# A depthwise convolution in two half-width phases, VectorE in program order during the attention, and later LayerNorms and weights, in a one-core encoder step

## The chip, the core and the metric

The kernel runs on one core of a Trainium2 chip. Of that core it uses TensorE (matrix products), VectorE, ScalarE and GpSimd (elementwise work; GpSimd also starts transfers that add to their target) and SyncE, which starts most transfers. The page of the profile calls them PE, DVE, ACT, POOL and SP; PEld is TensorE's loading of weights. The metric is the time of one execution on the chip in microseconds (us), smaller is better, given as the median of several runs.

## The reference, cut to what matters

One step of a hybrid encoder layer for 1040 prompt tokens (16 learned ones and 1024 frames) and 32 tokens of a running stream, all in float32.

```python
glu, q, k, v = project(rmsnorm(x, norm_mix), w_in)      # glu = a * sigmoid(b), 512 channels
glu_ext = concat([conv_state, glu])                     # 30 earlier rows in front
y = depthwise_causal_conv(glu_ext, dw_w, dw_b)          # 31 taps for each channel, plus bias
a_out = silu(layernorm(y) * ln_g + ln_b)                # over the 512 channels
attn = chunked sliding-window attention(q, k, v, bias, sinks)
x = x + concat([a_out, attn]) @ w_out
x = x + conv_ffn(x)                                     # up, 3 taps, swish gate, down
return rmsnorm(x), caches
```

The convolution at issue is, for every channel c and token t, y[t, c] = bias[c] + sum over k from 0 to 30 of w[k, c] * glu_ext[t + k, c].

## The kernel before, in words

**Layout.** Channels lie on the 128 partitions and tokens run along the free dimension. The 1072 tokens are worked in three token blocks, b = 0, 1, 2 (TB, OB: 336 or 324, 384 and 352 columns). The 512 convolution channels are four channel blocks, p = 0 to 3. `glu[:, p]` holds the convolution's input, `acc[:, p]` its output (ACCW = 1102 columns, with a gap between prompt and stream). A product in full precision is made of three matmuls, with each operand split into a rounded high part and a residue (`mm3`, L252 to L257); `split` (L248 to L250) makes the high part with a cast on ScalarE and the residue with a subtraction on VectorE. `wsplit` (L237) does it for weights.

**Order of the work.** 
1. Input projections for all columns but the last channel block (`in_group`, L646); `in_evac` (L566) puts the results into place on VectorE, gating included.
2. The loop of the attention (L1007 to L1042), 20 steps: a job enters per step (1 for the learned tokens, 16 chunks, and the stream's at step 12). In a step, the job that entered the step before gets its softmax finished (`soft_b`, L767: a reciprocal and four multiplications, of which the last SCA[i] run on ScalarE, L774, and the others on VectorE, L772); the new job gets its scores (TensorE), bias and maximum (`softmax_a`, L757, VectorE) and exponentials (L764, ScalarE); then come the outputs of the job before last (`outs`, L837), the transposes of the last one (`trans`, L821), its copies (`probs`, L828) and `keep` (L845). FILL[i] pieces of the last channel block's projection fill the step (`stream`; 48 pieces, 7 done ahead of the loop). When they are through, `after_glu` (L942) splits the attention's result, two channel groups at a time (`ca_split`, L931), and the first matmuls of the attention's half of the output projection are made (`ahs`). For the two entries in CSD, `ca_split` makes the residues not on VectorE but as a negated copy on ScalarE (L936) and a transfer of GpSimd's that adds the source to it.
3. The attention's half of the output projection: 20 groups of 12 matmuls (L1118 to L1135). After every third matmul comes a `tick` (L1095), which drives the three LayerNorms (`ln`, L1050, one for each token block): the first starts at tick LN0 = 14, each next one LNS = 21 ticks after the one before it started, if no tap that it needs is left. In `ln`, `squared` notes that its sum of squares is through. After the group in which all three are noted, `open_cv` (L1108) opens the buffers CVH and CVL, and the LayerNorms may go on to their last step, the split into them (L1084 to L1087). If that has not come about by the end of the groups, L1136 to L1140 finish it there.
4. The rest of the convolution half's weights (L1141 to L1143), and `conv_half` (L1155) for each token block: eight outputs, each of 12 matmuls, added to X by VectorE (L1165), squared and split.
5. The feed-forward part, from L1203 on, which the change doesn't touch.

**The taps.** When a channel block's columns are there, `taps_of` (L616) puts a convolution into the queue `tapq`, one entry for each segment in SEGS: blocks 1 and 2 are one segment each of all three token blocks (1090 columns), block 0 is two, block 3 is three, one for each token block. An entry is 31 instructions on VectorE (`conv_taps`, L395 to L410): one multiplication with the bias added (the profile has it at L400) and 30 that multiply and add (L403). `taps(us)` (L434) takes taps from the queue, from its first two entries in turn (WAYS = 2), and charges each (columns + 120) / 960 us until the budget is used. In the attention the budget of step i is TA[i]; in phase 3 it is TH = 5.9 for each group.

**What sets the order.** In the regions `tc.manual_schedule(engines=MANUAL)` TensorE and ScalarE run their instructions in the order of the program. All other engines' orders come from a planner that simulates the timeline; taps are issued in `tc.high_priority(offset=-1000000)`, so that everything else goes ahead of them, and behind the instruction named in `issue_after` (in the attention, the last score operation of the step). MANEND is MANUAL with VectorE and is used at the kernel's end.

Of the kernel before, what the change touches and what calls it, by code (L numbers as in the profile page):

```python
# [11 lines left out]
F32 = mybir.dt.float32  # L12
# [39 lines left out]
NPB = 8  # L52
TGS = [3.0, 3.0, 1000.0, 1000.0]
TGW = [3.0, 5.0, 6.5, 3.5, 1000.0, 1000.0, 5.0, 1000.0, 1000.0, 1000.0, 3.5, 3.5, 1000.0, 1000.0, 1000.0, 1000.0, 1000.0, 1000.0, 3.0, 3.0, 1000.0, 1000.0, 1000.0, 1000.0, 1000.0, 1000.0, 7.0, 3.5, 3.5, 3.5]
TA = [2.01, 2.74, 5.63, 6.64, 4.22, 3.28, 2.42, 2.68, 2.08, 1.57, 2.08, 2.08, 3.18, 1.41, 2.1, 0.85, 4.71, 3.21, 5.98, 2.57]
TH = 5.9
WAYS = 2
BS = ((0, 2), (1, 0), (2, 1), (2, 2))
# [11 lines left out]
WLD = True  # L70
MANUAL = {mybir.EngineType.PE, mybir.EngineType.Activation}
MANEND = MANUAL | {mybir.EngineType.DVE}
SCA = [1, 2, 2, 2, 1, 1, 2, 2, 2, 2, 2, 1, 2, 2, 0, 1, 1, 2, 2, 2]
LN0 = 14
LNS = 21
FILL = [4, 6, 6, 2, 3, 3, 6, 1, 3, 3, 1, 4, 5, 0, 3, 6, 0, 3, 0, 3]
ORDER = [2, 3, 8, 9, 4, 5, 10, 11, 12, 13, 6, 7]
CHAINS = ((0, 1),)
# [2 lines left out]
CHK = 21  # L81
CHT = 0
CHG = (1, 2)
SEGS = (((0,), (1, 2)), ((0, 1, 2),), ((0, 1, 2),), ((0,), (1,), (2,)))
CSD = ['12', '00']
AH = (1, 2, 1, 3, 5, 4, 5)
AG = (('00', '02'), ('h',), ('l',), ('10',), ('12',))
AT = (1, 8)
# [81 lines left out]
def body(nc, tc, cp, wp, xp, dp, io):  # L170
# [22 lines left out]
    def pcol(name, i):  # L193
        o, _ = PRM[name]
        return prm[:, o + i:o + i + 1]
# [196 lines left out]

    tapq, spare = [], [0.0, 0]

    def conv_taps(p, a0, a1, b):  # L395
        e, a = glu[:, p, :], acc[:, p, a0:a1]

        def tap(k):
            if k == 0:
                nc.vector.tensor_scalar(out=a, in0=e[:, a0:a1], scalar1=pcol("cw", p * CW), scalar2=pcol("cb", p),  # L400
                                        op0=ALU.mult, op1=ALU.add)
            else:
                nc.vector.scalar_tensor_tensor(out=a, in0=e[:, a0 + k:a1 + k], scalar=pcol("cw", p * CW + k),  # L403
                                               in1=a, op0=ALU.mult, op1=ALU.add)

        ks = list(range(CW))
        if (p, b) in CHAINS:
            ks = [0, *range(CHK, CW)]
            chq.append([p, a0, a1, list(range(1, CHK))])
        tapq.append([b, a1 - a0, tap, ks, p])  # L410
# [225 lines left out]
    def flush():  # L636
        undefer()
        while pend and pend[0][1] in ready:
            c, b, ps = pend.pop(0)
            if c % 2:  # L640
                undefer()
            in_evac(c, b, ps)
            if c < 8 and c % 2:
                taps_of(c // 2, b)
# [54 lines left out]
    def fetch():  # L699
        if wsrc:  # L700
            raws.append(wraw(wsrc.pop(0)))
# [302 lines left out]
    left = (len(order) - NPRE) * 3 * KD - PF  # L1004
    for _ in range(PF):
        next(stream)
    for i in range(len(jobs) + 2):  # L1007
        job = jobs[i] if i < len(jobs) else None
        if a:
            a.soft_b(SCA[i])  # L1010
        if job:
            job.scores()
            job.soft_a()
            job.exps(0)
            job.exps(1)
        if z:
            z.outs()
        if a:
            a.trans()
            a.probs()  # L1020
        if z:
            z.keep()
            kept[0] = i - 2
        for _ in range(min(FILL[i], left)):
            next(stream)
            left -= 1
        flush()
        taps(TA[i], (job or a or z).q[1][3])
        if not left and not pend and not defer:
            for _ in stream:  # L1030
                pass
            next(later, None)
            ticks = len(jobs) + 2 - i
            for _ in range(AH[-ticks] if ticks <= len(AH) else 0):
                next(ahs, None)
            for q in adds:
                ah_add(*q)
            adds.clear()
        if i == CHE:
            with tc.issue_after(job.q[1][3]):  # L1040
                chain_end()
        z, a = a, job  # L1042
    for _ in later:
        pass
    for _ in ahs:
# [90 lines left out]
    if not CVH:  # L1136
# [1 line left out]
        while len(squared) < 3:  # L1138
            tick()
        open_cv()  # L1140
    for m2 in WOC[1:]:  # L1141
        whl[m2] = halves(take((None, None, *wres)[m2], WLD))
        fetch()  # L1143

    close(cS)
    cH, ph = pool("h3", "right")
# [8 lines left out]
    def conv_half(b, rms):  # L1155
        t0, n = OB[b]
        at = t0 - H0
        for i, m in enumerate(2 * h + j for h in WOC for j in range(2)):
            hi, lo = whl[m // 2][m % 2]
            ps = mmt()[:, :n]  # L1160
            for k in range(4):
                mm3(ps, [k], lambda k: hi[:, k, :], lambda k: lo[:, k, :], lambda k: CVH[b][:, k, :],
                    lambda k: CVL[b][:, k, :], k == 0, k == 3)
                tick()
            nc.vector.tensor_tensor(out=X[b][:, m, :], in0=X[b][:, m, :], in1=ps, op=ALU.add)  # L1165
            sq_sum(X[b][:, m, :], rb[b][:, :n], acc[:, i % 4, t0:t0 + n], i, nc.gpsimd)
            gsplit(BH[:, m, at:at + n], BL[:, m, at:at + n], X[b][:, m, :], pcol("g2", m))
            if i % 2:
                nc.sync.dma_start(xd[:, m - 1:m + 1, at:at + n], X[b][:, m - 1:m + 1, :])
            if rms and i in RS:  # L1170
                next(rms)
        for _ in rms or ():
            pass
# [724 lines left out]
```

## Time and profile before

| what | value |
|---|---|
| median of 3 runs | 1048.87 us (1048.4 to 1048.88) |
| the profiled execution | 1049.94 us |
| its span | 1048.2 us |
| instructions | 19994 |
| mean TensorE clock granted | 0.999 |

The profile is of one execution. Its page lists busy times, a chain of the work that ended last, and groups of instructions by line. The views beside it answer from the same trace: the waits of an engine (who waited, who released it, total, how often, the longest), busy time in stretches of time, and a timeline (start in us, how long the row lasts, engine, line, operation, output and inputs, size, how many instructions the row joins; in brackets the idle time before it and who ended it). Consecutive instructions of a kind are one row. The matmuls' ends are modelled, and they overlap, so a matmul's time is not its pace.

| stage | from to (us) |
|---|---|
| attention loop | 163.8 to 248.4 |
| attention's half of the output projection | 248.4 to 293.1 |
| first matmul of the convolution half | 293.1 |

### The profile page before, as it was taken

The page shows a single profiled execution, that of the slowest core. Times are in us where ns is not written, and L with a number is a line of the kernel's source. Part 1 is how long each engine was busy: PE and PEld are TensorE (multiplying, and loading weights), DVE is VectorE, ACT ScalarE, POOL GpSimd, SP SyncE. Part 2 cuts the span into 40 slices and gives each one's busy share as a digit, 9 for nine tenths or more (in the row PEclk, how much of TensorE's full clock was granted, in tenths as well). Part 3 has the DMA queues.
Part 4 walks back from the last instruction along what each step waited for, and adds up shares of the span by engine and source line. Part 5 has one row for each costly group of instructions (what it writes and reads, how often), then busy time and mean ns, then how long its engine had stood idle before and what let it go on. Part 6 is the DMA issues. An engine that isn't in the chain of part 4 may idle for free.

```text
span 1048.2 us, 19994 instructions
## 1 busy us (share of the span) xinstructions
PE 1030.8 (98%) x7747; PEld 1004.9 (96%) x7747; DVE 864.8 (83%) x1649; ACT 506.6 (48%) x1074; POOL 163.0 (16%) x205
## 2 busy tenths in 40 slices
PE   9999999989999999999999999999999999999997
PEld 8999998758999999999999999999999999999997
DVE  7999988899978978888887888888777976986636
ACT  8653336896676744433333443343336722532334
POOL 1133220002325220001000000110010041000043
PEclk9999999999999999999999999999999999999999
DMA  7378673124963123243233233332426795832204
GB/s 268 90 170 163 146 152 81 41 54 70 174 151 108 61 71 102 72 141 96 72 110 125 63 103 109 97 103 76 130 63 207 250 194 132 249 123 69 94 2 166
DMA packets 69047, 124.41 MB, mean 119 GB/s; under 512 B 10448, under 2 KB 42568, under 8 KB 68952
## 3 DMA queue, kind: packets, MB, share of 16 engines
q1 hardware_dynamic: 56392, 97.77, 29.2%
q0 software_dynamic: 12128, 24.95, 14.1%
q8 instruction: 61, 1.00, 0.4%
q10 hardware_dynamic: 432, 0.41, 0.1%
q14 instruction: 34, 0.28, 0.1%
HBM read 79.42 MB, written 27.51 MB: 102 GB/s over the span
## 4 chain that ended last, share of the span: by engine, by line
PE 88%; ACT 6%; DVE 3%; DMA 2%; issue 1%; DVEq 0%; ACTq 0%
PE mm L1282 55%; PE mm L255 10%; PE mm L256 10%; PE mm L257 10%; ACT pb L764 1%; DVE acc L403 1%; ACT glu L828 1%; DMA raw<-woc 1%; PE R L292 1%; ACT hi L341 1%; PE R L271 1%; DMA xs<-xT 0%; ACT glu L764 0%; ACT pb L774 0%; DMA prm<-prm 0%
## 5 line engine op out<-in xcount | busy, mean ns | idle before, releaser
L1282 PE MATMUL mm<-bh,sl 128*128 128x264 f32 (+1 forms) x912 | 214.0, 284 | 0.0
L1282 PEld LDWEIGHTS mm<-bh,sl 128*128 128x128 f32 x912 | 157.2, 188 | 0.0
L403 DVE SCALAR_TENSOR_TENSOR acc<-glu,prm,acc 128x324 f32<-128x324 f32 (+4 forms) x190 | 155.0, 844 | 1.1
L1282 PE MATMUL mm<-bl,sl 128*128 128x264 f32 (+1 forms) x424 | 120.9, 285 | 0.0
L1282 PE MATMUL mm<-th,rawr 128*128 128x264 f32 x640 | 120.0, 284 | 0.0
L1282 PE MATMUL mm<-bh,wlo 128*128 128x264 f32 (+1 forms) x440 | 117.6, 284 | 0.0
L1424 DVE TENSOR_TENSOR x<-x,mm 128x264 f32<-128x264 f32 (+7 forms) x238 | 76.5, 347 | 45.6 <-PE mm L1282 45.4
L1282 PE MATMUL mm<-bh,whi 128*128 128x264 f32 (+1 forms) x440 | 112.5, 284 | 0.0
L255 PE MATMUL mm<-hi,whi 128*128 128x352 f32 (+3 forms) x312 | 104.0, 333 | 0.0
L256 PE MATMUL mm<-lo,whi 128*128 128x352 f32 (+3 forms) x312 | 101.2, 324 | 0.2 <-DVE lo L342 0.2
L257 PE MATMUL mm<-hi,wlo 128*128 128x352 f32 (+3 forms) x312 | 101.2, 324 | 0.0
L1282 PEld LDWEIGHTS mm<-th,rawr 128*128 128x128 f32 x640 | 100.4, 188 | 0.0
L1282 PE MATMUL mm<-th,sl 128*128 128x264 f32 x352 | 92.7, 284 | 0.0
L1282 PE MATMUL mm<-tl,rawr 128*128 128x264 f32 x320 | 90.8, 284 | 0.0
L1282 PEld LDWEIGHTS mm<-bh,wlo 128*128 128x128 f32 x440 | 80.6, 188 | 0.0
L1282 PEld LDWEIGHTS mm<-bl,sl 128*128 128x128 f32 x424 | 79.9, 188 | 0.0
L1282 PEld LDWEIGHTS mm<-bh,whi 128*128 128x128 f32 x440 | 79.0, 188 | 0.0
L1282 PE MATMUL mm<-bl,whi 128*128 128x264 f32 (+1 forms) x272 | 77.5, 285 | 0.0
L1218 ACT CAST sl<-x 128x512 fp32r<-128x512 f32 (+1 forms) x41 | 29.7, 727 | 74.2 <-DMA x<-wup 41.0
L1282 PEld LDWEIGHTS mm<-th,sl 128*128 128x128 f32 x352 | 63.8, 188 | 0.0
L1282 PEld LDWEIGHTS mm<-tl,rawr 128*128 128x128 f32 x320 | 60.3, 188 | 0.0
L255 PEld LDWEIGHTS mm<-hi,whi 128*128 128x128 f32 x312 | 58.7, 188 | 1.2 <-issue 0.6
(400 smaller groups left out, 2923.1 us busy)
## 6 DMA issues: line engine op xcount, KB each, us to landing
x<-wup SPq DMA_DIRECT2D x20, 512.0 KB, 4.3
x<-wup SPq DMA_DIRECT2D x40, 256.0 KB, 2.8
yq<-x SPq DMA_DIRECT2D x32, 264.0 KB, 2.8
wlo<-raw POOLq DMA_DIRECT2D x16, 512.0 KB, 4.6
ca<-ca POOLq DMA_DIRECT2D x18, 383.0 KB, 5.2
raw<-win SPq DMA_DIRECT2D x12, 512.0 KB, 4.5
raw<-wdn SPq DMA_DIRECT2D x12, 512.0 KB, 4.6
rb<-yq SPq DMA_DIRECT2D x10, 528.0 KB, 5.0
```

What stands on the lines that cost most here:

```text
L255: nc.tensor.matmul(ps, whi(k), xhi(k), start=first and i == 0, stop=False)
L256: nc.tensor.matmul(ps, whi(k), xlo(k), start=False, stop=False)
L257: nc.tensor.matmul(ps, wlo(k), xhi(k), start=False, stop=last and i == n - 1)
L271: nc.tensor.matmul(ss[:, i:i + 1], z[:, at:at + P], ones[:, 0:1], start=j == 0, stop=j == len(parts) - 1)
L292: nc.tensor.matmul(R[:, at:at + P], left[i], diag[i], start=True, stop=True)
L341: hid[b, k] = nc.scalar.activation(HI[b][:, k, :], X[b][:, k, :], AF.Copy, scale=pcol("g1", k)).ins
L403: nc.vector.scalar_tensor_tensor(out=a, in0=e[:, a0 + k:a1 + k], scalar=pcol("cw", p * CW + k), in1=a, op0=ALU.mult, op1=ALU.add)
L764: nc.scalar.activation(qs_[i], qs_[i], AF.Exp, bias=m[0][:, i:i + 1], scale=-1.0, accum_out=m[1][:, i:i + 1])
L828: nc.scalar.copy(ptb[kv], pts[kv])
L1218: nc.scalar.copy(hi, raw)
L1282: nc.tensor.matmul(ps, w[:, j, :], x[:, j, :], start=first and j + i == 0, stop=j == 3 and i == 2, skip_group_check=True)
L1424: summed[0] = nc.vector.tensor_tensor(out=z, in0=z, in1=ps[:, lo_:hi_], op=ALU.add).ins
```

## The change

There are four edits.

- **Paired convolution.** For block 1, block 2 and the second segment of block 3 (`PAIRS`), even and odd output columns are computed apart, from even and odd inputs and from their sums. With S[i] = glu[2i+1] + glu[2i+2], 15 taps of odd weights on S are shared by both phases; 16 more for each phase use the differences of neighbouring weights on every second column (`pdif`, made by GpSimd once at the start). That is 48 instructions of half the columns in place of 31: one sum, 15 shared ones, which all add to the odd columns' accumulator, and 32 that alternate between the even and the odd columns. The sums are kept in places of `acc` and `glu` that are free at that time. Block 3 now has two segments, token block 0 (plain, 31 taps) and token blocks 1 and 2 together.
- **VectorE in program order in the attention.** The loop lies in a region MANEND, so that VectorE's instructions run as written there. `taps` moves ahead of `flush`. TA is new (steps 12 to 17 get 1.9 and 0.9), SCA gives four multiplications of steps 12 to 17 to VectorE that ScalarE had, and CSD is empty, so that all residues of the attention's split are made by VectorE.
- **LayerNorms further apart.** LNS is 24.
- **The last weights.** `conv_weights` for WOC[3] is called inside `conv_half` of token block 0 ahead of its fifth output, no longer ahead of the first.

```diff
-TA = [2.01, 2.74, 5.63, 6.64, 4.22, 3.28, 2.42, 2.68, 2.08, 1.57, 2.08, 2.08, 3.18, 1.41, 2.1, 0.85, 4.71, 3.21, 5.98, 2.57]
+TA = [2.01, 2.74, 5.63, 6.64, 4.22, 3.28, 2.42, 2.7, 2.5, 2.3, 2.4, 2.4, 1.9, 0.9, 0.9, 0.9, 0.9, 0.9, 3.0, 3.0]
-SCA = [1, 2, 2, 2, 1, 1, 2, 2, 2, 2, 2, 1, 2, 2, 0, 1, 1, 2, 2, 2]
+SCA = [1, 2, 2, 2, 1, 1, 2, 2, 2, 2, 2, 1, 1, 1, 0, 1, 0, 1, 2, 2]
-LNS = 21
+LNS = 24
-SEGS = (((0,), (1, 2)), ((0, 1, 2),), ((0, 1, 2),), ((0,), (1,), (2,)))
-CSD = ['12', '00']
+SEGS = (((0,), (1, 2)), ((0, 1, 2),), ((0, 1, 2),), ((0,), (1, 2)))
+PAIRS = ((1, 0), (2, 0), (3, 1))
+NP2 = CW // 2
+CSD = []
...
+    nc.gpsimd.tensor_tensor(out=pdif[:, :, 0], in0=wv[:, :, 2::2], in1=wv[:, :, 1::2], op=ALU.subtract)
+    nc.gpsimd.tensor_tensor(out=pdif[:, :, 1], in0=wv[:, :, 0:CW - 1:2], in1=wv[:, :, 1::2], op=ALU.subtract)
+    def pair_place(p, n):
+        return (None, acc[:, 3, ACCW - n:], acc[:, 3, 0:n], glu[:, 2, 0:n])[p]
+    def pair_taps(p, a0, a1, b):
+        n = (a1 - a0) // 2
+        sums = pair_place(p, n + NP2 - 1)
+        y = [acc[:, p, a0 + i:a1:2] for i in range(2)]
+        def e(k, m=n):
+            return glu[:, p, a0 + k:a0 + k + 2 * m - 1:2]
...
+            if i == 0:
+                m = n + NP2 - 1
+                nc.vector.tensor_tensor(out=sums, in0=e(1, m), in1=e(2, m), op=ALU.add)
+            elif i == 1:
+                w, x = pcol("cw", p * CW + 2 * j + 1), sums[:, j:j + n]
+                if j == 0:
+                    nc.vector.tensor_scalar(out=y[1], in0=x, scalar1=w, scalar2=pcol("cb", p), op0=ALU.mult,
+                                            op1=ALU.add)
+                else:
+                    one(y[1], x, w, y[1])
+            elif i == 2:
+                w = pcol("cw", p * CW) if j == 0 else pdif[:, p - 1, 0, j - 1:j]
+                one(y[0], e(2 * j), w, y[0] if j else y[1])
+            else:
+                w = pdif[:, p - 1, 1, j:j + 1] if j < NP2 else pcol("cw", p * CW + CW - 1)
+                one(y[1], e(2 * j + 1), w, y[1])
+        ks = [(0, 0), *((1, j) for j in range(NP2)), *((i, j) for j in range(NP2 + 1) for i in (2, 3))]
+        tapq.append([b, n, tap, ks, p])
...
+    region.__exit__(None, None, None)
+    region = tc.manual_schedule(engines=MANEND)
+    region.__enter__()
     for i in range(len(jobs) + 2):
...
+        taps(TA[i], (job or a or z).q[1][3])
         flush()
-        taps(TA[i], (job or a or z).q[1][3])
...
+    region.__exit__(None, None, None)
+    region = tc.manual_schedule(engines=MANUAL)
+    region.__enter__()
     for _ in later:
...
-    for m2 in WOC[1:]:
+    def conv_weights(m2):
         whl[m2] = halves(take((None, None, *wres)[m2], WLD))
         fetch()
+
+    for m2 in WOC[1:3]:
+        conv_weights(m2)
...
         for i, m in enumerate(2 * h + j for h in WOC for j in range(2)):
+            if b == 0 and i == 4:
+                conv_weights(WOC[3])
```

More of the change, by code (lines that the diff above doesn't have):

```diff
@@ L393, in body, with one, tap @@
     tapq, spare = [], [0.0, 0]
+    pdif = cp.tile([P, NCV - 1, 2, NP2], F32, tag="pdif", name="pdif")
+    co = PRM["cw"][0] + CW
+    wv = prm[:, co:co + (NCV - 1) * CW].rearrange("p (a b) -> p a b", b=CW)
+    nc.gpsimd.tensor_tensor(out=pdif[:, :, 0], in0=wv[:, :, 2::2], in1=wv[:, :, 1::2], op=ALU.subtract)
[8 more added lines that the diff above has]
+            return glu[:, p, a0 + k:a0 + k + 2 * m - 1:2]
+        def one(out, x, w, into):
+            nc.vector.scalar_tensor_tensor(out=out, in0=x, scalar=w, in1=into, op0=ALU.mult, op1=ALU.add)
+        def tap(k):
+            i, j = k
+            if i == 0:
+                assert not any(q[4] == p - 1 and (p == 3 or len(q[3]) > 2 * (NP2 + 1)) for q in tapq if q[2] is not tap)
+                m = n + NP2 - 1
[15 more added lines that the diff above has]
+        tapq.append([b, n, tap, ks, p])
     def conv_taps(p, a0, a1, b):
+        if (p, b) in PAIRS:
+            pair_taps(p, a0, a1, b)
+            return
         e, a = glu[:, p, :], acc[:, p, a0:a1]
```

## The prediction, made before the changed kernel was timed

> **What bounds the kernel now.** I read the page first, then who waited for whom on TensorE, then busy time by stretches of the attention.
>
> ```profile
> span 1048.2 us, 19994 instructions
> PE 1030.8 (98%) x7747; PEld 1004.9 (96%) x7747; DVE 864.8 (83%) x1649; ACT 506.6 (48%) x1074; POOL 163.0 (16%) x205
> ```
> ```profile
> PE o L837 <- ACT ca L845: 3.5, 9, 0.8
> PE mm L255 <- DVE x L1165: 1.9, 2, 1.7
> PE pt L821 <- ACT pb L774: 1.3, 2, 0.9
> ...
> PE pt L821 <- DVE glu L772: 1.0, 1, 1.0
> ```
> ```profile
> 220.00:230.00 10.00, 8.07 (x67) 5.45 (x67) 9.81 (x39) 10.00 (x32) 0.90 (x1) 1.00 0.40 71
> ```
>
> The first fence holds the page's first lines: TensorE is busy for 98% of the span and bounds the whole, so all that can be won or lost is where it waits. The second holds its longest waits (waiting instruction, who released it, total, count, longest): 5.8 us in the attention (3.5 + 1.3 + 1.0) and 1.9 us at the start of the convolution half of the output projection. The third is a stretch of the attention (TensorE 8.07 of 10 us, its weight loads 5.45, VectorE 9.81, ScalarE 10.00): ScalarE is full, which is why it is named in most waits; VectorE is just as full, but much of that is taps, which yield to everything else. So the change must be judged by what it does to TensorE's waits, not by how much work VectorE saves.
>
> **Part by part. (a) The paired convolution ahead of the attention.** Channel blocks 1 and 2 had 31 taps of 1090 columns; now 48 instructions of half the width (1 sum, 15 shared, 32 own).
>
> ```profile
> 107.55 4.12 DVE L403 SCALAR_TENSOR_TENSOR acc<-glu,prm,acc 128x1090 f32<-128x1090 f32 x3
> ```
> ```profile
> 195.91 0.37 DVE L757 CUSTOM_DVE_ANT_0 glu<-S,bt 128x209 f32<-128x209 f32 x1
> ...
> 200.93 1.14 DVE L403 SCALAR_TENSOR_TENSOR acc<-glu,prm,acc 128x324 f32<-128x324 f32 x2
> ...
> 203.13 0.55 DVE L582 SCALAR_TENSOR_TENSOR glu<-mm,glu 128x384 f32<-128x384 f32 x1
> 203.60 0.55 DVE L403 SCALAR_TENSOR_TENSOR acc<-glu,prm,acc 128x324 f32<-128x324 f32 x1
> 204.06 0.47 DVE L400 TENSOR_SCALAR acc<-glu,prm 128x384 f32<-128x384 f32 x1
> ```
>
> Two taps of 324 on the same accumulator took 1.14 us, so the second began 0.59 after the first (1.14 less the 0.55 of one), once that was over; a tap followed by something that doesn't read it gave way after 0.46 (203.60 to 204.06), 0.13 sooner. Chained 1090 taps take 4.12 / 3 = 1.37. By a line through 0.59 at 324 and 1.37 at 1090 a chained half-width one (545) takes 0.82, an alternating one 0.69. So 0.8 + 15 x 0.82 + 32 x 0.69 = 35.2 us replace 31 x 1.37 = 42.5, twice. This lies under TensorE's projections, where it waits for no tap; what shows is that block 2 no longer runs into the attention (the 1.0 us wait for VectorE above). I take -1.0, between -1.0 and 0. The 90 weight differences on GpSimd run once at the start: 0; without that cover, two small operations.
>
> All taps in the trace read with stride one; the new ones with stride two. Nothing here prices that. I take no extra; the other end, double time per column, is a rival. [...]
>
> **(b) Steps 7 to 11, VectorE in program order.** Block 3 comes late: its first third (columns 12 to 336) is ready in step 6 by FILL (32 pieces are needed; 7 before the loop and 4+6+6+2+3+3 make 31 by step 5, 37 by step 6), and since the budget is now spent before the evacuation, taps begin in step 7. TA charges a 324 tap 0.4625 us: 6, 6, 5, 5, 5 taps in steps 7 to 11, 27 in all, and none of another block to alternate with, as the rest of block 3 arrives at the end of step 11. So they run as a chain, 0.59 each, and in program order the next step's softmax stands behind them.
>
> ```profile
> 211.93 0.17 DVE L769 RECIPROCAL sm<-sm 128x4 f32<-128x4 f32 x1
> 212.13 0.81 DVE L772 TENSOR_SCALAR pb<-pb,sm 128x209 f32<-128x209 f32 x3
> 212.85 0.37 DVE L757 CUSTOM_DVE_ANT_0 glu<-S,bt 128x209 f32<-128x209 f32 x1
> ...
> 214.03 2.08 DVE L403 SCALAR_TENSOR_TENSOR acc<-glu,prm,acc 128x324 f32<-128x324 f32 x4
> ...
> 216.60 0.33 DVE L757 CUSTOM_DVE_ANT_0 pb<-S,bsm 128x177 f32<-128x177 f32 x1
> ```
>
> From step 7's first score operation (195.91) to step 12's (216.60) are 20.7 us now. In program order VectorE owes in that stretch: scores 5 x 1.18 (212.85 to 214.03) = 5.9; reciprocals 5 x 0.20 = 1.0; multiplications 2+2+2+3+3 = 12 x 0.24 (three from 212.13 to 212.85) = 2.9; taps 27 x 0.59, less 0.12 at each of five chain ends, = 15.3; two evacuations x 0.47 (203.13 to 203.60) = 0.9; four residues of the attention's split, priced like an evacuation, = 1.9 (CSD is empty, so two more than before, and all ahead of step 12's softmax). That is 27.9 us, so +7.2. Each step's transposes need that step's multiplications, so TensorE is held too. I take +7.2; the ends are +3.7 (taps at 0.46: 11.8 in place of 15.3) and +8.2 (0.2 more a step, for ScalarE's exponentials arriving late).
>
> [...]
>
> **(c) Steps 12 to 19.** Here VectorE has little left (TA gives 1 to 4 taps) and ScalarE sheds work.
>
> ```profile
> 216.66 0.48 ACT L936 ACTIVATE cal<-ca 128x324 fp32r<-128x324 f32 x1
> 217.04 0.45 ACT L935 CAST cah<-ca 128x324 fp32r<-128x324 f32 x1
> ...
> 218.48 0.83 ACT L774 ACTIVATE pb<-pb,sm 128x209 f32<-128x209 f32 x2
> 219.21 0.44 ACT L764 ACTIVATE pb<-pb,sm 128x177 f32<-128x177 f32 x1
> ```
>
> Four multiplications at 0.37 ((219.21 - 218.48) / 2) and four negated copies at 0.38 (216.66 to 217.04) leave ScalarE: -3.0. Against it stands a new wait: in steps 14 and 15 VectorE, in program order, waits for ScalarE's last cast, then does the residue (0.47), reciprocal (0.20), 3 or 4 multiplications (0.24 each) and the first score (1.18 / 4) before ScalarE may go on with its exponentials; it has at most one multiplication or a copy meanwhile. That is some 1 us of empty ScalarE twice. I take -1.0, between -3.0 and +0.5.
>
> **(d) The first LayerNorms.** 28 of block 3's 48 paired taps are left when the attention ends (48 less 20), and the second LayerNorm now needs them all (one segment instead of two).
>
> ```profile
> 244.34 4.83 DVE L403 SCALAR_TENSOR_TENSOR acc<-glu,prm,acc 128x384 f32<-128x384 f32 x9
> ...
> 258.36 1.70 DVE L1061 SCALAR_TENSOR_TENSOR acc<-S,acc 128x324 f32<-128x324 f32 x4 [0.81 <-PE S L1059]
> ```
> ```profile
> 248.41 0.44 PE L255 MATMUL mm<-cah,whi 128*128 128x384 f32 x1
> ```
> ```profile
> 269.21 0.81 PE L1059 MATMUL S<-glu,ones 128*128 128x384 f32 x2
> ```
>
> 28 x 0.53 ((4.83 - 0.6) / 8) = 14.8; the last four residues at the evacuation's 0.47, 1.9; ten operations of the first LayerNorm at 1.70 / 4, 4.3; three sums 1.4; small ones some 0.5: 22.9 us, and VectorE idled 0.8 in there: 23.7. TensorE reaches the second mean 269.21 - 248.41 = 20.8 us after the attention today. LNS = 24 puts it three ticks later; 80 ticks fill the 44.65 us from 248.41 to 293.06 (row in (e)), 0.56 each: 22.5. I take +1.0, between 0 and +3 (the taps at the chained 0.59 or more).
>
> **(e) The convolution half starts late.** 80 ticks, one per three matmuls, drive the LayerNorms: they begin at 14, 14 + LNS, 14 + 2 LNS, and 16 ticks later each is counted. The third is counted at 56 + 16 = 72 now, at the end of the third last group; with 24 at 62 + 16 = 78, inside the last. The buffers CVH open after that group, so block 0's casts fall behind the two weight takes in ScalarE's program order.
>
> ```profile
> 293.61 1.05 ACT L240 CAST wrh<-raw 128x1024 fp32r<-128x1024 f32 x1
> 294.56 1.05 ACT L240 CAST whi<-raw 128x1024 fp32r<-128x1024 f32 x1
> 302.48 1.05 ACT L240 CAST wrh<-raw 128x1024 fp32r<-128x1024 f32 x1 [6.87 <-DMA raw<-woc]
> 303.43 1.75 ACT L249 CAST cvh<-acc 128x384 fp32r<-128x384 f32 x4
> 305.08 0.47 ACT L297 ACTIVATE rb<-x 128x324 f32<-128x324 f32 x1
> ```
> ```profile
> 293.06 0.31 PE L255 MATMUL mm<-cvh,whi 128*128 128x324 f32 x1
> ```
>
> TensorE goes on with cvh at 293.06, before ScalarE's two weight takes start at 293.61: today the casts are done by then. After the change the first cast starts at 295.5 (294.56 + 0.95) and ends 0.41 later ((305.08 - 303.43) / 4), at 295.9; VectorE's residue ends as much later, or, behind the second weight's own residue, some 1 us after that, at about 297.3. So TensorE waits 3.2 to 4.2 us with nothing else to do: I take +3.7.
>
> **(f) The last weights.** The 1.9 us wait came from VectorE standing behind the cast at 302.48 with TensorE's evacuations queued after it; conv_weights(3) now comes after four outputs. I take -1.3: some 0.6 stays, as ScalarE then reaches that cast after four squares and splits, close to the need. Ends -1.9 and 0.
>
> **Sum:** -1.0 + 7.2 - 1.0 + 1.0 + 3.7 - 1.3 = +8.6 us. Against the profiled execution's own 1049.94 us (1.74 around the span) that is 1058.5; the timed runs' median, 1048.87, lies 1.07 lower, so 1057.5. All lower ends together, -1.0 + 3.7 - 3.0 + 0 + 3.2 - 1.9, make +1.0, all upper ends, 0 + 8.2 + 0.5 + 3.0 + 4.2 + 0, +15.9: 1049.9 to 1064.8 for this case, with little chance at the far ends.
>
> **Rivals.** First, the taps yield as before: they carry the lowest priority, and if that outranked the region's program order, (b) would be 0 and (c) its full -3.0. With (a) -1.0, (d) 0, (e) 3.2 and (f) -1.9 that is -2.7, so 1046.2, faster. It decides where taps stand behind the next step's scores. Against it: the casts at 303.43 carry the same low priority on an engine already kept in program order, and ran ahead of L297, as written. Chance 0.16.
>
> Second, chained taps run at 0.46 like the others, where one that waits for the tap before it loses nothing: (b) +3.7, and (c) -2.0, as VectorE arrives earlier; with the other terms -1.0 + 3.7 - 2.0 + 1.0 + 3.7 - 1.3 = +4.1, so 1053.0. The two chained rows speak against it. [...] Chance 0.12.
>
> Third, stride two doubles a column's time. The line above gives 0.00102 us a column, so 47 of 48 instructions gain 0.56 in blocks 1 and 2 and, with 383 columns, 0.39 in block 3: 2 x 26.3 + 18.3, less the 2 x 7.3 saved in (a), some +56, about 1105. No row bears on it. Chance 0.03.
>
> **Numbers.** My forecast has the other 0.69; 2.1 us, 0.2%, is about what a measurement of this kernel can tell from no change. The range goes from just under the first rival to the forecast's upper bounds less a tail: 1046 to 1063. Faster by more than that takes most of the first rival and a sliver of the rest: 0.15; within it, the first rival's rest and the lower ends of forecast and second: 0.15; slower 0.70. Alone, my forecast has 1051 to 1063.
>
> **What would show it.** (b): VectorE's taps in chains of five or six in steps 7 to 11, scores over 5 us apart, TensorE's transposes waiting for VectorE. (c): ScalarE idle after the casts of steps 14 and 15. (e): block 0's casts behind two weight casts and TensorE idle over 3 us before the first cvh matmul. (f): no long wait at the seventh output. I am wrong if TensorE's waits in the attention stay at 5.8 us or fall, or if a half-width tap lasts over 0.9 us.

## The result and the profile after

The changed kernel takes 1067.14 us (median of 4 runs, 1066.28 to 1067.4) against 1048.88 (1048.4 to 1050.0): a ratio of 1.0167, 95% interval 1.0152 to 1.0182, or 18.3 us slower. The forecast had the direction, but its 1057.5 was 9.6 us too low and its range ended at 1063. The profiled execution took 1067.4 us, its span is 17.4 us longer than before.

The first lines of the page:

```profile
span 1065.6 us, 20011 instructions
PE 1037.6 (97%) x7747; PEld 1010.1 (95%) x7747; DVE 851.4 (80%) x1677; ACT 505.5 (47%) x1066; POOL 158.6 (15%) x205
```

VectorE works 13.4 us less (864.8 before) and the kernel is slower: what the paired convolution saves was not on the path. TensorE has the same 7747 matmuls, yet is busy for 6.8 us longer (1030.8 before), so waits cannot be all. First the waits of TensorE (lines of the changed kernel are some 48 higher; L885 was L837, L869 was L821, L257 was L255):

```profile
PE o L885 <- ACT ca L893: 5.6, 10, 1.3
PE mm L257 <- ACT cvh L251: 2.8, 1, 2.8
PE pt L869 <- DVE pb L820: 2.7, 3, 1.0
PE pt L869 <- DVE glu L820: 2.4, 2, 2.0
PE mm L257 <- ACT wrh L242: 1.4, 1, 1.4
PE mm L258 <- DVE cvl L252: 1.1, 1, 1.1
...
PE mm L258 <- DVE cal L252: 0.8, 2, 0.6
PE mm L259 <- DVE wrl L244: 0.8, 1, 0.8
...
PE S L273 <- DVE glu L1121: 0.7, 1, 0.7
```

The waits in the attention grew from 5.8 to 10.7 us on these lines (5.6 + 2.7 + 2.4), with VectorE named in 5.1 of them where it was 1.0. The start of the convolution half waits 3.9 (2.8 + 1.1) and its seventh output 2.2 (1.4 + 0.8). Then the stretches around three of these waits, five us each; after the stretch's bounds come its length, the busy time of TensorE, its weight loads, VectorE, ScalarE and GpSimd, and then the clock granted to TensorE:

```profile
235.00:240.00 5.00, 3.58 (x27) 2.54 (x27) 2.81 (x14) 4.40 (x15) 0.00 (x0) 1.00 0.39 105
240.00:245.00 5.00, 4.16 (x21) 3.77 (x19) 4.81 (x20) 3.19 (x13) 0.00 (x0) 0.66 0.02 5
300.00:305.00 5.00, 2.21 (x17) 1.92 (x15) 2.01 (x6) 3.70 (x7) 2.15 (x3) 1.00 0.60 81
305.00:310.00 5.00, 3.92 (x15) 3.69 (x16) 2.82 (x6) 1.88 (x6) 0.00 (x0) 0.66 1.01 259
320.00:325.00 5.00, 3.36 (x15) 3.11 (x16) 2.69 (x5) 4.78 (x9) 1.52 (x3) 0.82 0.64 192
```

Here is what the forecast left out. Behind each of the three long waits the clock is lower: by stretches of one us it lies at 0.50 for about 3.4 us each time (241 to 245, 306 to 310, 323 to 327), which is 1.7 us of clock lost each, 5.1 in all. In the profiled execution of the kernel before it was 1.00 up to the last microseconds. These are single executions: the four of the changed kernel have mean clocks of 0.994 and 0.991, and the two with 0.991 (1067.1 and 1067.2 us) lie between the two with 0.994 (1066.3 and 1067.4), so clock lost is not always time lost.

Where the time went is found by looking up the same matmul in both timelines (the n-th that reads a given operand). Of the kernel before, and then of the changed one:

```profile
219.01 0.33 PE L821 MATMUL pt<-ident,pb 128*128 128x128 f32 x1 [0.88 <-ACT pb L774]
...
292.11 0.32 PE L255 MATMUL mm<-cah,whi 128*128 128x352 f32 x1
...
309.84 0.31 PE L257 MATMUL mm<-cvh,wrl 128*128 128x324 f32 x1
```
```profile
222.99 0.29 PE L869 MATMUL pt<-ident,pb 128*128 128x128 f32 x1
...
300.96 0.41 PE L257 MATMUL mm<-cah,whi 128*128 128x352 f32 x1
...
326.37 0.45 PE L259 MATMUL mm<-cvh,wrl 128*128 128x324 f32 x1
```

They are 3.98, 8.85 and 16.53 us later. With three more such pairs (172.32 and 171.74, 251.13 and 257.55, 297.66 and 311.84) this gives a ledger by the steps of the forecast:

| step | lateness at its end | its share | forecast |
|---|---|---|---|
| (a) paired convolution, to 172 us | -0.6 | -0.6 | -1.0 |
| (b) steps 7 to 11, to step 12's transposes | +4.0 | +4.6 | +7.2 |
| (c) steps 12 to 19 | +6.4 | +2.4 | -1.0 |
| (d) first LayerNorms, to 292 us | +8.9 | +2.4 | +1.0 |
| (e) start of the convolution half | +14.2 | +5.3 | +3.7 |
| (f) last weights | +16.5 | +2.4 | -1.3 |
| the rest | +17.4 | +0.9 | 0 |

### The profile page after: what moved, and what is told of

It is laid out like the page before. It is cut to its first block, busy times and chain, and to the rows that moved or that the text cites. A ratio compares the mean times of both kernels' runs of the same rounds, so it can differ in the third digit from the quotient of the medians.

```text
span 1065.6 us, 20011 instructions
## 1 busy us (share of the span) xinstructions
PE 1037.6 (97%) x7747; PEld 1010.1 (95%) x7747; DVE 851.4 (80%) x1677; ACT 505.5 (47%) x1066; POOL 158.6 (15%) x205
## 4 chain that ended last, share of the span: by engine, by line
PE 86%; DVE 7%; ACT 4%; DMA 2%; issue 1%; DVEq 0%; ACTq 0%
PE mm L1341 52%; PE mm L257 9%; PE mm L259 9%; PE mm L258 9%; DVE acc L451 1%; DVE acc L415 1%; DMA gx<-yq 1%; ACT pb L812 1%; PE R L294 1%; ACT hi L343 1%; DVE bl L1278 1%; ACT glu L876 1%; PE R L273 1%; DVE cal L252 1%; DMA xs<-xT 0%
## 5 line engine op out<-in xcount | busy, mean ns | idle before, releaser
L257 PE MATMUL mm<-hi,whi 128*128 128x352 f32 (+3 forms) x312 | 104.0, 333 | 0.0
L415 DVE SCALAR_TENSOR_TENSOR acc<-glu,pdif,acc 128x545 f32<-128x545 f32 (+1 forms) x90 | 59.9, 724 | 0.0
L257 PEld LDWEIGHTS mm<-hi,whi 128*128 128x128 f32 x312 | 58.6, 188 | 1.0 <-issue 0.6
```

Of the source, the lines that this page charges most:

```text
L257: nc.tensor.matmul(ps, whi(k), xhi(k), start=first and i == 0, stop=False)
L415: nc.vector.scalar_tensor_tensor(out=out, in0=x, scalar=w, in1=into, op0=ALU.mult, op1=ALU.add)
```

## The experiments

The theory after this reading: VectorE in program order costs the attention, as chained taps and residues stand ahead of the next softmax; LNS = 24 costs the start of the convolution half; and each long wait of TensorE costs again as much as half of 3.4 us of lower clock. The rivals: the third LayerNorm is late whatever LNS says; the new budgets and shares cost the attention in any order; half-width instructions with stride two are dear; the fall of the clock has another reason or costs nothing.

All times are medians; the kernel before had 1048.84 to 1049.31 beside them, and the ratios are to it.

**lns21 and lns21_weights.**

```diff
-LNS = 24
+LNS = 21
```
```diff
-    for m2 in WOC[1:3]:
+    for m2 in WOC[1:]:
         conv_weights(m2)
...
-            if b == 0 and i == 4:
-                conv_weights(WOC[3])
```

The first diff alone is lns21, both are lns21_weights.

> The changed kernel with LNS = 21 again, all else as changed. Theory (LNS = 24 puts token block 0's casts behind two weight takes on ScalarE, so that TensorE waits 3.9 us at the start of the convolution half, and its granted clock then falls to about half for 3.4 us, which costs 1.7 more): both go, 1067.1 - 5.6 = 1061.5 us, with the clock at 1.00 at the start of the convolution half. Rival (the third LayerNorm is late because VectorE is behind, whatever LNS says): the wait stays, 1065 us or more.

Measured 1060.47 us, ratio 1.0104 (1.0087 to 1.0120). ScalarE's timeline of the changed kernel, and then of lns21:

```profile
302.55 1.05 ACT L242 CAST wrh<-raw 128x1024 fp32r<-128x1024 f32 x1
303.50 1.05 ACT L242 CAST whi<-raw 128x1024 fp32r<-128x1024 f32 x1
304.44 1.55 ACT L251 CAST cvh<-acc 128x324 fp32r<-128x324 f32 x4
```
```profile
300.02 1.55 ACT L251 CAST cvh<-acc 128x324 fp32r<-128x324 f32 x4
...
303.60 1.05 ACT L242 CAST wrh<-raw 128x1024 fp32r<-128x1024 f32 x1
304.54 1.05 ACT L242 CAST whi<-raw 128x1024 fp32r<-128x1024 f32 x1
```

The casts are ahead of the weight takes again, no wait for cvh is left and the clock is 1.00 from 306 to 310. LNS = 24 is worth 6.7 us here, a little more than expected; the rival falls. The single executions lie between 1059.4 and 1061.6 us, so differences of 1 us between such kernels say little.

> As lns21, and the last weights taken ahead of the convolution half again, as before the change. Theory (taken inside, that cast and its residue stand behind squares and splits that wait for VectorE; TensorE waits 2.2 us there and the clock falls once more, 1.7): these 3.9 go and the 1.9 us of before come back, so 2.0 less than lns21, 1059.5 us. Rival (the move is a gain of 1.3, as forecast, and only the late start spoils it): 1.3 more than lns21, 1062.8 us.

Measured 1059.33 us, ratio 1.0094 (1.0078 to 1.0109): 1.1 less than lns21, where the theory had 2.0 and the rival 1.3 more. The executions of the two overlap (1058.0 to 1059.7 here), so this shows no gain of moving the last weights, even with the start mended, and no sure loss.

**weights_ahead_24.** The second diff alone.

> The changed kernel with LNS = 24 kept and only the last weights taken ahead of the convolution half again. Theory (with LNS = 24 token block 0's casts stand behind all weight takes, and the third take waits for its transfer, which landed 8.9 us after the first cast in the kernel before): the first cvh matmul comes some 7 us later than in the changed kernel, and its later 2.2 us wait and clock loss go: 1067.1 + 4 = 1071 us. Rival (the place of the last weights matters by itself, as in lns21_weights): 1066 us or less.

Measured 1068.33 us, ratio 1.0184 (1.0168 to 1.0199), 1.2 more than the changed kernel. The first of TensorE's waits:

```profile
PE mm L257 <- ACT cvh L251: 9.4, 1, 9.4
```

The wait at the start is longer by 6.6 us (9.4 for 2.8), near the expected 7, but much of that comes back: the 2.2 us at the seventh output and what the clock lost there. The size was missed, 1.2 for 4; yet the rival (1066 or less) fails too. With LNS = 24 moving the weights is at best a small gain, as the intervals of the two ratios overlap, and neither place is good.

**dve_planner.** Program order off in the attention, all else as changed.

```diff
-    region = tc.manual_schedule(engines=MANEND)
+    region = tc.manual_schedule(engines=MANUAL)
     region.__enter__()
     for i in range(len(jobs) + 2):
```

> The changed kernel with VectorE's order in the attention left to the planner again; TA, SCA, CSD, the place of the taps and all else as changed. Theory (the program order costs the attention, with chained taps standing ahead of the next step's scores): the attention is 6 to 8 us shorter and the clock stays up in it, 1059 to 1061 us. Rival (the new budgets and residues load VectorE whatever its order): the attention stays within 2 us, 1065 us or more.

Measured 1059.18 us, ratio 1.0094 (1.0079 to 1.0109): program order is worth 8.0 us of the changed kernel, as the theory had it. The matmul of 251.13 stands at 251.11 (257.55 in the changed kernel), and the clock stays at 1.00 in the attention; the rival falls.

**pairs_alone.** Paired convolution and block 3's two segments in the kernel before; the other lines as they were.

```diff
-SEGS = (((0,), (1, 2)), ((0, 1, 2),), ((0, 1, 2),), ((0,), (1,), (2,)))
+SEGS = (((0,), (1, 2)), ((0, 1, 2),), ((0, 1, 2),), ((0,), (1, 2)))
+PAIRS = ((1, 0), (2, 0), (3, 1))
```

> The kernel before with the paired convolution alone (block 3 in two segments with it); TA, SCA, CSD, LNS, the order of taps and evacuation, VectorE's planner and the weights as before. Theory (half-width instructions cost what the forecast said, 35 us for a block in place of 42, under TensorE's work): 1047.9 to 1049 us, no TensorE wait for VectorE at 172 us. Rival (block 3's 48 instructions, needed as a whole by the second LayerNorm, hold the LayerNorms up): 1051 us or more, with the wait at the first cvh matmul.

Measured 1049.88 us, ratio 1.0005 (0.9995 to 1.0014): no difference. That is above the theory's 1047.9 to 1049 and below the rival's 1051. The wait at 172 us is gone and the matmul there comes 0.7 us sooner, but by the matmul of 251.13 this kernel is 0.6 us late. Its clock fell in the attention, though no wait of TensorE there was longer than 1.0 us and the whole is not measurably slower:

```profile
220.00:225.00 5.00, 4.28 (x23) 2.69 (x23) 4.41 (x16) 5.00 (x16) 0.00 (x0) 0.66 0.26 41
```

The half-width instructions cost what the forecast said (VectorE of the changed kernel):

```profile
104.11 2.87 DVE L415 SCALAR_TENSOR_TENSOR acc<-glu,pdif,acc 128x545 f32<-128x545 f32 x4
```

Four that alternate between two accumulators take 2.87 us, 0.70 apart with 0.78 for the last (the forecast: 0.69). Four of the shared ones, which form a chain, take 3.25 us at 80.33, 0.82 apart, as forecast. Stride two adds nothing here: the forecast's line through taps with stride one gives 0.69 and 0.82.

**planner_lns21.** dve_planner with the two diffs of lns21_weights: budgets, shares and place of the taps are what is left of the change beside the pairs.

> As pairs_alone with the new TA, SCA, CSD and the taps ahead of the evacuation (so the changed kernel without program order, LNS = 24 and the moved weights). Theory (the new shares give VectorE residues that come late at the end of the attention, worth the 2.5 us seen in dve_planner by 264 us): 1049.9 + 2.5 = 1052.4 us. Rival (LNS and the weights are all of dve_planner's loss): 1050.4 us or less.

Measured 1052.92 us, ratio 1.0032 (1.0019 to 1.0044): 3.0 more than pairs_alone, the theory's 2.5 nearly met. Three waits that the kernel before didn't have:

```profile
PE pt L940 <- DVE pb L820: 2.1, 1, 2.1
...
PE mm L258 <- DVE cal L252: 0.8, 2, 0.6
...
PE S L273 <- DVE glu L1121: 0.7, 1, 0.7
```

L940 are the transposes of the stream's job in step 13. Of its two multiplications, both on ScalarE before, SCA now gives one to VectorE. This longest wait is not where the time goes, though: the matmul of 251.13 is 0.8 us late, in pairs_alone 0.6. The 3.0 us stand behind the attention, where the late residues (cal) and a sum (L273) wait for VectorE: by the matmul of 292.11 this kernel is 3.9 late, pairs_alone 0.4.

**order_alone.** The kernel before with the region MANEND around the loop and nothing else.

> The kernel before with the loop of the attention in a region in which VectorE runs in program order too, and nothing else changed. Theory (program order itself makes the taps stand ahead of scores, whatever the convolution is): slower by 4 to 7 us, 1053 to 1056 us. Rival (only the new budgets make it dear; the old ones were cut to fit the steps): within 1.5 us of 1049.1.

Measured 1057.43 us, ratio 1.0081 (1.0066 to 1.0096): 8.6 us slower, above the expected 4 to 7. Program order is dear with the old budgets too; the rival falls.

**fewer_chained.** lns21_weights with half of the taps of steps 7 to 11 moved behind step 12.

```diff
-TA = [2.01, 2.74, 5.63, 6.64, 4.22, 3.28, 2.42, 2.7, 2.5, 2.3, 2.4, 2.4, 1.9, 0.9, 0.9, 0.9, 0.9, 0.9, 3.0, 3.0]
+TA = [2.01, 2.74, 5.63, 6.64, 4.22, 3.28, 2.42, 1.3, 1.2, 1.2, 1.2, 1.2, 1.9, 1.4, 2.0, 2.0, 2.0, 2.0, 4.0, 4.0]
```

> As lns21_weights (VectorE in program order), with TA of steps 7 to 11 cut to 1.3 and four times 1.2, and steps 13 to 19 raised: 14 taps in steps 7 to 11 in place of 27, none left out. Theory (the chained taps ahead of the next step's scores are what program order costs in steps 7 to 11): 13 x 0.59 = 7.7 us less for VectorE there, ScalarE's pace decides again, and of the 4.9 us that TensorE had lost by step 12 at least 4 come back; after step 12, 13 more taps fill VectorE's idle time and cost at most 1: 1059.3 - 3 to 4 = 1055 to 1056 us. Rival (it is the order of softmax and residues that costs, not the taps): 1058.5 us or more.

Measured 1054.67 us, ratio 1.0053 (1.0038 to 1.0068): 4.7 less than lns21_weights. Program order costs 6.4 there (lns21_weights less planner_lns21, which differ in nothing else), so the chained taps are the larger part of it. Some of the 4.7 may be the clock's: the profiled execution of lns21_weights lost 5.1 us of clock in the attention (221 to 229 and 241 to 246), that of fewer_chained none.

**old_shares.** lns21_weights with SCA and CSD of before.

> As lns21_weights, with SCA and CSD as before the change (four multiplications and four residues back on ScalarE, two of the residues finished by transfers). Theory (in program order the residues stand ahead of the softmax of steps 12, 16 and 17, and TensorE waits for them): 2 us less, 1057.3 us, with the 2.0 us wait of step 12 gone. Rival (ScalarE's relief is worth its 3 us, as taken at most in the forecast): 2 us more, 1061.3 us.

Measured 1058.07 us, ratio 1.0087 (1.0072 to 1.0102), 1.3 less. The sign is the theory's, but the executions overlap (1057.8 to 1059.0, and 1058.0 to 1059.7), and the profiled one lost 3.4 us less clock; that the wait of step 12 would go was wrong. VectorE and TensorE there:

```profile
221.16 0.90 DVE L252 TENSOR_TENSOR cal<-ca,cah 128x324 fp32r<-128x324 f32 x2 [0.79 <-ACT cah L251]
...
222.57 0.33 PE L869 MATMUL pt<-ident,glu 128*128 128x128 f32 x1 [2.12 <-DVE glu L820]
```

There are two residues in place of four, but in program order VectorE now stands still for ScalarE's casts, which come behind two more negated copies; the softmax is as late as before.

**fewer_chained_old_shares.** Fewer chained taps and the old shares together.

```diff
+TA = [2.01, 2.74, 5.63, 6.64, 4.22, 3.28, 2.42, 1.0, 0.9, 0.9, 0.9, 0.9, 0.9, 1.9, 2.0, 1.9, 1.0, 2.0, 4.0, 5.0]
```

> VectorE in program order, LNS = 21 and the weights ahead as in lns21_weights, SCA and CSD of before, and about 2 chained taps in each of steps 7 to 11. Theory (the two savings seen apart, 4.7 us for the taps and 1.3 us for the shares, add up): 1059.3 - 6.0 = 1053.3 us. Rival (with the taps out of the way ScalarE is the bound, and the shares' work is worth having off it): 1054.7 us or more.

Measured 1056.88 us, ratio 1.0074 (1.0061 to 1.0088): they don't add up; it is 2.2 slower than fewer_chained. Its attention is not slower (the matmul of 251.13 comes at 251.69, in fewer_chained at 251.96), but the LayerNorms behind it wait longer for VectorE (2.3 us at the means, L1113, for 1.4). The rival's time is met (1054.7 or more), but not by its mechanism, which lay in the attention. Since this TA also puts more taps behind step 12, the run doesn't tell shares from taps; that stays open.

**keep_warm and keep_warm12.** dve_planner with 24, or 12, matmuls of ones by ones in the wait at the start of the convolution half.

```diff
     for b in range(3):
         for _ in lns[b]:
             pass
+        if b == 0:
+            for _ in range(24):
+                nc.tensor.matmul(pts[0][:, 0, 0:P], ones, ones, start=True, stop=True)
         conv_half(b, ...)
```

> As dve_planner, with 24 matmuls of ones by ones (128 columns, into a bank that nothing reads) on TensorE ahead of the convolution half's first matmul, where TensorE waits 2.8 us. Theory (the granted clock falls because TensorE stood still, and the 3.2 us that dve_planner loses after that wait are the clock's): the clock stays at 1.00 there, the wait itself stays, 1059.2 - 3.2 = 1056.0 us. Rival (the clock falls for another reason, such as the load of the matmuls since, or the fall costs nothing): 1059 us or more, by the time of the 24.

Measured 1057.9 us, ratio 1.0085 (1.0068 to 1.0102), 1.3 less than dve_planner. The 24 took 5.3 us and overran the wait, so a gain of the clock and a loss of time are mixed in it; keep_warm12 parts them.

> As keep_warm, with 12 of the matmuls of ones, which fill 2.6 us and so lie within the 2.8 us wait (the 24 took 5.3 us and overran it). Theory (what follows the wait at the halved clock costs about 3 us, and matmuls in the wait save them): 1059.2 - 3.2 = 1056.0 us, the first cvh matmul within 0.3 us of where dve_planner has it (298.5) and the clock at 1.00 after it. Rival (the fall is not worth that; keep_warm's 1.3 us are all there is): 1057.9 us or more.

Measured 1056.53 us, ratio 1.0072 (1.0058 to 1.0086): 2.65 less than dve_planner for twelve matmuls more (each has two records in the trace). TensorE in dve_planner, then in keep_warm12 (timelines), and the stretch from 300 us in the same order:

```profile
298.51 0.64 PE L257 MATMUL mm<-cvh,whi 128*128 128x324 f32 x1 [2.79 <-ACT cvh L251]
```
```profile
295.56 2.84 PE L1250 MATMUL pt<-ones 128*128 128x128 f32 x24
298.52 0.42 PE L257 MATMUL mm<-cvh,whi 128*128 128x324 f32 x1
```
```profile
300.00:305.00 5.00, 5.00 (x22) 5.00 (x23) 1.79 (x5) 1.52 (x5) 0.00 (x0) 0.62 0.76 242
```
```profile
300.00:305.00 5.00, 4.99 (x33) 4.99 (x34) 3.23 (x8) 2.97 (x9) 0.00 (x0) 1.00 0.77 245
```

The first cvh matmul comes at the same time; what differs is the clock after it, 0.62 or 1.00, and so 22 matmuls in five us or 33. The fall didn't come where TensorE had work in the wait, so here it followed from TensorE standing still. By the matmul of 297.66 keep_warm12 is 1.7 us ahead of dve_planner, by that of 309.84 2.4 us, as the wait for wrh at the seventh output is shorter too (0.5 for 1.2).

**after_keep_warm.** The changed kernel with 12 matmuls of ones at the same place and 6 ahead of the seventh output.

> The changed kernel with matmuls of ones in two of its waits: 12 ahead of the convolution half's first matmul and 6 ahead of its seventh output. Theory (each of these waits is followed by 3.4 us at half clock, 1.7 us lost each): the clock stays at 1.00 after both, the waits stay, 1067.1 - 3.4 = 1063.7 us, a little more where the 6 overrun. Rival (the clock costs nothing beyond the waits): 1067 us or more.

Measured 1062.71 us, ratio 1.0127 (1.0113 to 1.0141): 4.4 less than the changed kernel, 1.0 more than expected. The clock stays at 1.00 after both waits. In the profiled executions 0.8 us are won by the matmul of 251.13, in the attention, where the fall now lies at 222 to 226 us and no longer at 241 to 245, though nothing was put in there. A further 1.4 are won at the start of the convolution half (e) and 2.4 at the last weights (f), where the wait is also 0.9 us shorter (from the last matmul before it to the first on wrl, 316.79 to 318.99 in place of 319.05 to 322.19).

**pairs_three_moved and pairs_seven_moved.** pairs_alone, and multiplications moved to VectorE where it may let taps wait: three in steps 12, 16 and 17, and four more in steps 7 to 10.

```diff
-SCA = [1, 2, 2, 2, 1, 1, 2, 2, 2, 2, 2, 1, 2, 2, 0, 1, 1, 2, 2, 2]
+SCA = [1, 2, 2, 2, 1, 1, 2, 2, 2, 2, 2, 1, 1, 2, 0, 1, 0, 1, 2, 2]
```

> As pairs_alone (planner, LNS = 21), with three of the four multiplications of steps 12, 16 and 17 moved from ScalarE to VectorE, the one of the stream's job in step 13 left on ScalarE. Theory (ScalarE's pace decides in these steps, and the taps make way): 3 x 0.37 = 1.1 us less than pairs_alone, 1048.8 us. Rival (VectorE is as full as ScalarE there, so nothing is won): 1049.9 us.

Measured 1048.66 us, ratio 0.9996 (0.9987 to 1.0005), 1.2 less than pairs_alone, as the theory had it, but no measurable gain on the kernel before. Where taps yield, work moved off ScalarE is thus worth its price in these steps.

> As pairs_three_moved, with one more multiplication moved from ScalarE to VectorE in each of steps 7 to 10. Theory (ScalarE's pace decides there too, and taps yield): 4 x 0.37 = 1.5 us less, 1047.2 us. Rival (VectorE is full there and the multiplications wait behind a tap that is running): 1048.7 us or more.

Measured 1049.07 us, ratio 0.9996 (0.9987 to 1.0005): the four more win nothing; the rival holds. No version here beats the kernel before.

## Why the prediction was too low, step by step

The runs split the 18 us in time as well: pairs 0.7 (1049.88 less the 1049.14 beside it, within the noise), budgets and shares 3.0, LNS and weights 6.3 under the planner, program order 8.0 on top.

**(a) held.** -0.6 for -1.0, and the prices of the half-width instructions with it. That stride two adds nothing was taken with no row to show it; the changed kernel's trace shows nothing added, 0.70 and 0.82 us against 0.69 and 0.82 by the line through stride one. The third rival is out.

**(b) held as a mechanism, and its sum on VectorE to 1%.** VectorE's timeline of the changed kernel:

```profile
195.15 0.38 DVE L805 CUSTOM_DVE_ANT_0 glu<-S,bt 128x209 f32<-128x209 f32 x1 [2.31 <-PE S L850]
...
216.93 2.92 DVE L451 SCALAR_TENSOR_TENSOR acc<-glu,prm,acc 128x324 f32<-128x324 f32 x5
219.77 0.58 DVE L630 SCALAR_TENSOR_TENSOR glu<-mm,glu 128x320 f32<-128x320 f32 x2
220.26 1.71 DVE L252 TENSOR_TENSOR cal<-ca,cah 128x324 fp32r<-128x324 f32 x4
221.88 0.17 DVE L817 RECIPROCAL sm<-sm 128x4 f32<-128x4 f32 x1
...
222.81 0.34 DVE L805 CUSTOM_DVE_ANT_0 pb<-S,bsm 128x177 f32<-128x177 f32 x1
```

From step 7's first score to step 12's are 27.7 us; the forecast summed 27.9. Five chained taps take 2.92, 0.59 apart. So the second rival is out: in this chain a tap took 0.59, against the 0.46 of a tap whose result the next doesn't read (203.60 to 204.06 in the kernel before). The first rival, that the taps yield, is out too: the taps of 216.93 stand ahead of the reciprocal of 221.88. What yielding taps are worth is what dve_planner shows: 8 us. What failed is that TensorE was charged all of VectorE's 7.2: it lost 4.6. Before, step 12's transposes came 2.4 us behind its first score (216.60 and 219.01), and now they come 0.2 behind it (222.81 and 222.99). The forecast's lower end has a slip: 27 taps at 0.46 are 12.4 us and not 11.8, so that end was +4.3, and the second rival 1053.6.

**(c) failed.** It set "some 1 us of empty ScalarE twice" against a gain of 3.0. The wait that was named is there, but larger, and it starts a chain. VectorE, then ScalarE:

```profile
239.43 1.03 DVE L252 TENSOR_TENSOR cal<-ca,cah 128x384 fp32r<-128x384 f32 x2 [2.19 <-ACT cah L251]
```
```profile
234.78 0.47 ACT L822 ACTIVATE pb<-pb,sm 128x209 f32<-128x209 f32 x1 [0.83 <-DVE sm L817]
235.85 0.47 ACT L812 ACTIVATE pb<-pb,sm 128x209 f32<-128x209 f32 x1 [0.60 <-DVE sm L805]
...
241.94 0.47 ACT L812 ACTIVATE pb<-pb,sm 128x209 f32<-128x209 f32 x1 [1.81 <-DVE sm L805]
```

VectorE stands 2.2 us for the casts, then ScalarE 1.8 for the scores that stand behind the residues, of which there are two here (1.03) where the forecast priced one (0.47). One step earlier ScalarE stands 0.83 and 0.60, so 3.2 in place of 2. TensorE has neither outputs nor transposes meanwhile, and its clock falls, with 1.7 us of clock lost by 245. How the rest of the 3.4 us between forecast and trace splits is open. Where taps yield, three of the four multiplications won 1.2 (pairs_three_moved), so program order is the likely reason why relieving ScalarE won nothing here; that isn't shown by a run of its own.

**(d) failed in its place**, 2.4 for 1.0. The forecast had TensorE wait for VectorE at the second mean; no such wait is in the trace. TensorE waits for VectorE's late residues (cal, 0.8) and for a sum (L273, 0.7) instead. planner_lns21 has the same two waits and loses 3.1 in this stretch, so they belong to the new budgets, shares and place of the taps, whatever the order; how they split between these wasn't settled.

**(e) held as a mechanism.** The wait was 3.9 for 3.7 (2.8 + 1.1), with the casts behind two weight takes. What it cost was more, because half clock followed for 3.4 us: with the wait filled (after_keep_warm) this stretch loses 3.9 and not 5.3.

**(f) failed in sign.** The forecast named "some 0.6" of wait. The wait is 2.2, and the clock falls again. ScalarE of the changed kernel:

```profile
318.87 0.48 ACT L301 ACTIVATE acc<-x 128x324 f32<-128x324 f32 x1 [3.33 <-DVE x L1224]
319.25 0.55 ACT L305 ACTIVATE bh<-x,prm 128x324 fp32r<-128x324 f32 x1
319.71 1.03 ACT L242 CAST wrh<-raw 128x1024 fp32r<-128x1024 f32 x1
```

In ScalarE's program order the cast now stands behind work that waits 3.3 us for VectorE's additions; TensorE stands for these weights from 319.4 (its matmul starts at 320.79 after 1.43 us of waiting).

**The step that failed over all of them** is the first sentence on what bounds the kernel: "all that can be won or lost is where it waits". It priced each wait at its own length and the clock behind it at nothing. By the granted clock 5.1 us were lost so, and after_keep_warm won back 4.4 with two of three places filled. The span went 8.8 us beyond the forecast's 8.6. With each fall put at its 1.7 us, the 3.7 that are not the clock's are (c) 1.7, (d) 1.4, (f) 2.0 and small ones 1.2, less the 2.6 that (b) had too many; so one error hid part of the others.

Two of these shares are rough. In after_keep_warm (f) loses nothing (0.0 for 2.4), so there the falls cost more than their own clock. And the fall in the attention can't be taken at 1.7: five kernels have the same program in the attention and differ in where the fall lies. The matmul of 251.13 is 5.6 to 5.7 us late where it lies at 222 to 227 (after_keep_warm, weights_ahead_24), 6.4 where it lies at 241 to 245 (the changed kernel), and 6.7 to 6.9 where the clock is down at 221 to 229 and at 241 to 246 (lns21_weights, lns21). What the fall costs against none at all is not shown.

## What to carry to other kernels

Where TensorE is the bound, price a wait of two or three us not at its length alone: look at how busy TensorE is in the few us around it, and add, as an estimate, half of the time for which the clock may be down (in the changed kernel TensorE had 0.4 to 1.4 us of work in the three us before each fall, and 3.4 us at 0.50 followed, 1.7 us of clock; in planner_lns21 3.4 us of clock lost cost 0.8). Putting an engine in program order turns every operation of low priority on it into a wait for those behind (8.0 us in the changed kernel, 8.6 in order_alone); a budget for such work must be priced at its chained pace and fit into the slack of that very step. An edit that takes work from a full engine won 1.2 us here where taps yield (pairs_three_moved), and in program order taking it back (old_shares) cost nothing; so see first whether the engine that gets the work is waited for at that place. Two edits made for each other (here LNS and the late weights) should be taken back together before either is judged.

## What the runs showed of the hardware

The granted clock fell to 0.50 for 3.4 us or twice that, behind waits (10.2 us in weights_ahead_24, around its wait of 9.4). In the changed kernel no wait behind which the clock fell was as long as the 3.4 us of the fall: at the start of the convolution half TensorE waited 2.8 and 1.1 us with one matmul between. In the three us before its three falls (238, 303 and 320 us on) TensorE was busy for 1.1, 0.4 and 1.4 us, and before that of pairs_alone (218 us on) for 1.9. The same 2.1 us wait at step 13's transposes was followed by a fall in planner_lns21 (223 to 229 us) and by none in dve_planner; what decides between the two isn't shown. This fall cost less than its clock: in planner_lns21 3.4 us of clock were lost there (0.51 over 7 us), and the matmul of 251.13 is 0.8 us late, where dve_planner, which has the same program up to there and no fall, has it on time (251.11).
